# One stage of a four-layer trunk: the recurrence's first group in a fixed order, with its gate beside the value projection

## The chip, the core and the metric

The kernel runs on one core of a Trainium2 chip. The metric is device time in microseconds (us). The core has five engines that work side by side and wait for each other through semaphores: TensorE (PE, its weight loads PEld), VectorE (DVE), ScalarE (ACT), GpSimd (POOL) and SyncE (SP). SyncE and ScalarE also issue the transfers between HBM and the on-chip memory (SPq, ACTq). Each engine takes its own instructions in a fixed order. [...]

## The reference

A trunk of four layers over x and a context, 256 tokens of width 1024 each: a gated spatial layer (SGU), a bidirectional recurrent layer (RWKV-7), a latent attention layer (MLA) and a gated spatial layer again. The change lies in the recurrent layer alone. What it computes, cut to the parts that matter:

```python
r, k, v, z = (xs[e] @ w_in[e] for e in range(4))
log_w = -softplus(-(w0 + tanh(xs_w @ w_lora1) @ w_lora2)) - 0.5      # per direction n
decay = exp(-exp(log_w))
a     = sigmoid(a0 + (xs_a @ a_lora1) @ a_lora2)                      # per direction n
k_dir = k * (1 + (a - 1) * k_a)
kk    = normalize_per_head(k * k_k)
# for each token, each of 16 heads of 64, each of 2 directions:
S = S * w_t - (S @ kk_t) outer (kk_t * a_t) + v_t outer k_t
y_t = S @ r_t
out = ((norm(y_0 + y_1) + bonus(r, k_dir, v)) * silu(z)) @ w_out
```

The state is carried from the context's 256 tokens into x's 256, so the scan runs over 512 tokens.

## The kernel before

The scan is done in chunks of 64 tokens, 8 chunks, and in four groups `g` of four heads. A group has four lanes: two pairs of heads (`pr`) times two directions (`n`), lane = 2 n + pr. For each group there are these parts, each a Python generator that issues a piece of work and yields:

- `features(g)`, lane by lane (L700): the low-rank products `pw` and `pa` (L715, L716), a tanh of each on ScalarE (L730, L735), +1 on GpSimd (L731), a scan on VectorE (L739), two exponentials on ScalarE (`P` L741 and L742), then the operands of the scan's products: `AR` (L752, L753), `b` (L757), a scaling by `kab` on ScalarE (L758), and `BK`, its even rows on GpSimd (L767) and its odd rows on VectorE (L768). Their inputs k, r and kk were stored in HBM by the stage before and are fetched on SyncE's queue (L720), as are the low-rank weights (L707).
- `inverse(g)` (L778): TensorE's products `nab` (L789) and copies into `X`, a transpose on VectorE (L801), 31 pairs of dependent VectorE steps `tmp` and `Tm` (L806, L807), two transposes (L811, L813), and two rounds of small products `pg` and `px` (L826, L837).
- `operands` (`pe` L862 with its masks `E` L866, `pbk` L882) and `chain(g)` (L890): in each of 8 chunks `pz`, `pu`, `pd`, `py`, with the state `S` carried on.
- `gate(g)` (L959): the projection z as 32 products of 128x256 (`pg` L976; its tiles `xz` and `wz` tell it from the `pg` of the inverse) and a silu.

`values()` (L1068), once for the layer, is the projection of v: 64 products of 128x512 (`pv` L1076), the copy of each result (L1078), its flip in time (`prv` L1083), stores of both (L1091), and transposes (`vfm` L1096). Its weights come in four tiles `wv` of 1024 KB; two are fetched ahead of it (L1063).

Order: a scheduler places the instructions of each engine by its own costs, from the order in which the generators are interleaved. `interleave` (L115) takes from each flow in the ratio of the given numbers. The stage that the change rewrites is L1106, `values()` beside the features and the inverse of group 0; after it, the loop over `g` runs the chain of a group beside the features and inverse of the next one, the gate of its own, and the norm and output of what is done. In the trace, the stage runs from 543.4 us (first `pv`) to 656.6 us (first `pz`), the chain of group 0 to 748.6, that of group 1 to 850.8.

Tiles lie in pools: a pool with a tag has a number of buffers (`bufs`), and a tile that reuses a buffer waits until the old one was read. Pools that are closed give their space to later ones, so that tiles of two stages can lie over each other. The stage before (k and r projections) evacuates each result into a tile `ev` (L624) and stores it from ScalarE's queue (L626).

Of the kernel before, what the change touches and what calls it, by code (L numbers as in the profile page):

```python
# [8 lines left out]
F32 = mybir.dt.float32  # L9
F32R = mybir.dt.float32r  # L10
# [7 lines left out]
T = 512  # L18
# [80 lines left out]
def body(tc, I, out):  # L99
# [3 lines left out]
    V, S, PE = nc.vector, nc.scalar, nc.tensor  # L103
# [385 lines left out]
    def rwkv(m, tail):  # L489
# [182 lines left out]
        nc.gpsimd.memset(cmask[:, :, 0:1], 0.0)  # L672
        Pt = [st(f"P{i}", [128, 8, 65], 1) for i in range(2)]
# [26 lines left out]
        def features(g, f):  # L700
            f["12"] = st("12", [128, 4, 8], 3)
            for pr in range(2):
                o = g * 2 + pr
                w2 = {}
                for nm in "wa":
                    raw = st("f", [128, T], NF)[:, 0:256].rearrange("p (n c) -> p n c", n=2)
                    nc.sync.dma_start(out=raw, in_=I[f"rw_{nm}2"][:, :, o * 128:o * 128 + 128])  # L707
                    whi, wlo = st("w2" + nm, [128, 2, 128], 1, F32R), st("l2" + nm, [128, 128], 1, F32R)
# [5 lines left out]
                def second(p, nm, n):  # L714
# [3 lines left out]
                def fetch(nm, tag="f", n=NF):  # L718
                    t = st(tag, [128, T], n)
                    nc.sync.dma_start(out=t, in_=spill[nm, o])  # L720
                    return t

                ko, ro, kk = fetch("k"), fetch("r"), fetch("kk")
                kd = []
                for n in range(2):
                    lane = n * 2 + pr
                    pw = ps("pw", "f")
                    second(pw, "w", n)
                    tw = st("f", [128, T], NF)
                    S.activation(rev(tw, n), seg(pw), AF.Tanh, scale=0.5, bias=half[:, n, o:o + 1])  # L730
                    nc.gpsimd.tensor_scalar(tw, tw, 1.0, None, ALU.add)  # L731
                    pa = ps("pa", "f")
                    second(pa, "a", n)
                    ta = st("f", [128, T], NF)
                    S.activation(rev(ta, n), seg(pa), AF.Tanh, scale=0.5, bias=half[:, 2 + n, o:o + 1])  # L735
                    yield
                    c = st("f", [128, T], NF)
                    c8 = c.rearrange("p (c t) -> p c t", c=8)
                    V.tensor_tensor_scan(c, cmask.rearrange("p c t -> p (c t)"), tw, 0.0, ALU.mult, ALU.add)  # L739
                    P = Pt[n]  # L740
                    S.activation(P[:, :, 1:65], c8, AF.Exp, scale=-KAPPA2)  # L741
                    S.activation(c, c, AF.Exp, scale=KAPPA2)  # L742
                    nc.gpsimd.tensor_copy(f["12"][:, lane, :], P[:, :, 64])
                    yield

                    def r4(x):

                        return rev(x, n).rearrange("p s (c t) -> p s c t", c=4)

                    for sg in range(2):  # L750
                        ar = st(f"AR{sg}", [128, 4, 2, 64], 8)
                        V.tensor_tensor(ar[:, :, 0, :], r4(kk)[:, sg], P[:, sg * 4:sg * 4 + 4, 0:64], ALU.mult)  # L752
                        V.tensor_tensor(ar[:, :, 1, :], r4(ro)[:, sg], P[:, sg * 4:sg * 4 + 4, 1:65], ALU.mult)  # L753
                        f["AR"][lane, sg] = ar
                    yield
                    b = tw
                    V.scalar_tensor_tensor(out=seg(b), in0=seg(ta), scalar=1.0, in1=rev(kk, n), op0=ALU.add, op1=ALU.mult)  # L757
                    S.activation(ta, ta, AF.Identity, scale=half[:, 4, o:o + 1], bias=kab[:, o:o + 1])  # L758
                    yield
                    V.tensor_tensor(seg(ta), seg(ta), rev(ko, n), ALU.mult)  # L760
                    kd.append(ta)
                    b4, c4, k4 = (x.rearrange("p (s c t) -> p s c t", s=2, c=4) for x in (b, c, ta))
                    for sg in range(2):
                        bk = st(f"BK{sg}", [128, 9, 64], 8)

# [5 lines left out]
                V.tensor_tensor(seg(kd[0]), seg(kd[0]), rev(kd[1], 1), ALU.add)
                V.scalar_tensor_tensor(out=kd[0], in0=kd[0], scalar=hvec[:, 0, o:o + 1], in1=ro, op0=ALU.mult, op1=ALU.mult)
                if pr == 0:
                    spill["rk", g] = dp.tile([128, 2, T], F32, name=f"rk{g}")
# [702 lines left out]
```

## Time and profile before

| | us |
|---|---|
| median of 3 runs | 1611.42 (1608.29 to 1612.81) |
| profiled execution | 1612.92 |
| its span | 1611.1 |
| TensorE busy in the span | 1519.5 (94%) |
| VectorE, ScalarE, GpSimd busy | 1149.1, 795.2, 101.1 |
| mean granted clock of TensorE | 0.98 |

A row of the timeline gives start, length, engine, line, operation, tiles (out <- in) and how many such instructions were joined in it; in brackets the idle time of that engine just before and what ended it. A row of the windows gives, for a stretch of time, the busy time of each engine, TensorE's granted clock, the share of the transfer engines that was busy and GB/s. A 32-bit matmul leaves two records in the trace, so 16 records are 8 matmuls.

### The profile page before, as it was taken

The page shows a single profiled execution, that of the slowest core. Times are in us where ns is not written, and L with a number is a line of the kernel's source. Part 1 is how long each engine was busy: PE and PEld are TensorE (multiplying, and loading weights), DVE is VectorE, ACT ScalarE, POOL GpSimd, SP SyncE. Part 2 cuts the span into 40 slices and gives each one's busy share as a digit, 9 for nine tenths or more (in the row PEclk, how much of TensorE's full clock was granted, in tenths as well). Part 3 has the DMA queues.
Part 4 walks back from the last instruction along what each step waited for, and adds up shares of the span by engine and source line. Part 5 has one row for each costly group of instructions (what it writes and reads, how often), then busy time and mean ns, then how long its engine had stood idle before and what let it go on. Part 6 is the DMA issues. An engine that isn't in the chain of part 4 may idle for free.

```text
span 1611.1 us, 29355 instructions
## 1 busy us (share of the span) xinstructions
PE 1519.5 (94%) x11860; PEld 1181.4 (73%) x11860; DVE 1149.1 (71%) x2160; ACT 795.2 (49%) x1434; POOL 101.1 (6%) x135
## 2 busy tenths in 40 slices
PE   5999999999988998999998999799999999989998
PEld 2768888888966644776776777688777777768887
DVE  3769998864898377586887844778766666665876
ACT  4534331223665354345345332569866766356543
POOL 0000000000000132303213000000000000000000
PEclk9999999999999999899999999999999999989999
DMA  9766567742144652532433133134321222265452
GB/s 352 271 246 224 191 218 260 261 153 79 53 144 150 183 164 70 153 96 74 126 99 94 62 100 121 53 118 145 115 74 53 80 85 92 70 233 199 165 183 79
DMA packets 95176, 229.07 MB, mean 142 GB/s; under 512 B 26048, under 2 KB 52160, under 8 KB 80576
## 3 DMA queue, kind: packets, MB, share of 16 engines
q1 hardware_dynamic: 92736, 223.00, 40.8%
q10 hardware_dynamic: 2304, 4.20, 0.7%
q8 instruction: 93, 1.52, 0.4%
q14 instruction: 43, 0.35, 0.1%
HBM read 208.81 MB, written 17.83 MB: 141 GB/s over the span
## 4 chain that ended last, share of the span: by engine, by line
PE 47%; DVE 7%; ACT 5%; issue 1%; POOL 1%; DMA 0%; ACTq 0%; POOLq 0%; DVEq 0%
PE fm L323 5%; PE op L323 4%; PE pg L976 3%; PE fm L324 2%; PE op L1047 2%; PE op L324 2%; PE pz L323 2%; PE pu L323 2%; PE po L1358 2%; PE sc L1376 2%; PE pe L862 2%; PE sc L1377 1%; PE pv L416 1%; PE pv L417 1%; PE pz L324 1%
## 5 line engine op out<-in xcount | busy, mean ns | idle before, releaser
L191 DVE TENSOR_TENSOR lo<-raw,hi 128x2048 fp32r<-128x2048 f32 (+3 forms) x161 | 251.7, 1567 | 108.6 <-ACT hi L190 108.1
L190 ACT CAST hi<-raw 128x2048 fp32r<-128x2048 f32 (+3 forms) x161 | 212.1, 1324 | 226.9 <-PE op L327 40.6
L258 DVE SCALAR_TENSOR_TENSOR junk<-adaw,scb 128x1024 f32<-128x1024 f32 x112 | 136.7, 1221 | 10.0 <-DMA adaw<-in_ada_wT 8.1
L323 PE MATMUL op<-s,hi 128*128 128x512 f32 x256 | 91.6, 400 | 0.0
L415 PE MATMUL pv<-hi,hp 128*128 128x512 f32 x192 | 78.2, 409 | 9.1 <-ACT hi L190 6.0
L416 PE MATMUL pv<-lo,hp 128*128 128x512 f32 x192 | 77.7, 405 | 1.7 <-DVE lo L191 1.7
L323 PE MATMUL fm<-hx,hi 128*128 128x512 f32 x200 | 74.1, 411 | 4.1 <-ACT hx L317 3.8
L417 PE MATMUL pv<-hi,hp 128*128 128x512 f32 x192 | 77.2, 402 | 0.0
L324 PE MATMUL op<-s,lo 128*128 128x256 f32 x256 | 71.1, 280 | 0.0
L976 PE MATMUL pg<-xz,wz 128*128 128x256 f32 x256 | 70.2, 408 | 0.0
L767 POOL TENSOR_TENSOR BK<-f 64x256 f32<-64x256 f32 x64 | 57.3, 895 | 44.4 <-DVE f L760 27.4
L866 DVE TENSOR_TENSOR E<-pe,masks 128x512 f32<-128x512 f32 x64 | 41.5, 682 | 25.5 <-PE pe L862 23.0
L324 PE MATMUL fm<-hx,lo 128*128 128x256 f32 x200 | 56.7, 288 | 2.0 <-DVE lo L191 2.0
L323 PEld LDWEIGHTS op<-s,hi 128*128 128x128 f32 x256 | 48.1, 188 | 12.5 <-issue 1.3
L1076 PE MATMUL pv<-wv,xv 128*128 128x512 f32 x128 | 57.2, 596 | 0.0
L1047 PE MATMUL op<-Y,wo 128*128 128x256 f32 x192 | 55.8, 427 | 1.3 <-DVE xT L1051 1.3
L323 PE MATMUL fm<-cq,hi 128*128 128x512 f32 x144 | 55.7, 422 | 0.0
L976 PEld LDWEIGHTS pg<-xz,wz 128*128 128x128 f32 x256 | 47.0, 197 | 11.5 <-issue 3.8
L415 PEld LDWEIGHTS pv<-hi,hp 128*128 128x128 f32 x192 | 37.7, 197 | 19.4 <-ACT hi L190 6.6
L326 PE MATMUL pu<-hp,hi 128*128 128x512 f32 x128 | 51.1, 400 | 0.0
L327 PE MATMUL pu<-hp,hi 128*128 128x512 f32 x128 | 50.5, 395 | 0.0
L328 PE MATMUL pz<-hp,lo 128*128 128x512 f32 x128 | 50.5, 395 | 0.0
(413 smaller groups left out, 4088.2 us busy)
## 6 DMA issues: line engine op xcount, KB each, us to landing
adaw<-in_ada_wT SPq DMA_DIRECT2D x36, 1024.0 KB, 4.9
raw<-in_sgu_v SPq DMA_DIRECT2D x16, 1024.0 KB, 4.8
raw<-in_sgu_u SPq DMA_DIRECT2D x16, 1024.0 KB, 4.8
raw<-in_sgu_z SPq DMA_DIRECT2D x16, 1024.0 KB, 4.7
raw<-in_sgu_o SPq DMA_DIRECT2D x16, 1024.0 KB, 4.8
adaw<-in_ada_w SPq DMA_DIRECT2D x24, 512.0 KB, 9.6
xz<-xz SPq DMA_DIRECT2D x32, 256.0 KB, 4.2
raw<-in_ml_z SPq DMA_DIRECT2D x16, 512.0 KB, 3.6
```

Source lines behind the costliest of these rows:

```text
L190: S.copy(hi[:, sl], raw[:, sl])
L191: V.tensor_tensor(lo[:, sl], raw[:, sl], hi[:, sl], ALU.subtract)
L258: V.scalar_tensor_tensor(out=junk, in0=raw[:, f, :], scalar=1.0, in1=scb[:, c, :], op0=ALU.mult, op1=ALU.mult, accum_out=m[:, t * 2 + f, c ...
L323: PE.matmul(p, whi, x, start=start, stop=False)
L324: PE.matmul(p[:, 0:256], wlo, x[:, 0], start=False, stop=stop)
L415: PE.matmul(pv[tb], hs[k][:, 0, sl], whi[:, ws_], start=k == 0, stop=False)
L416: PE.matmul(pv[tb], hs[k][:, 0, sl], wlo[:, ws_], start=False, stop=False)
L417: PE.matmul(pv[tb], hs[k][:, 1, sl], whi[:, ws_], start=False, stop=k == 7)
L767: nc.gpsimd.tensor_tensor(bk[H[h], 2 * h:2 * h + 7:2, :], k4[H[h], sg], c4[H[h], sg], ALU.mult)
L976: PE.matmul(p, ws[k // 4][:, k % 4, pr * 128:pr * 128 + 128], xs[k // 2][:, k % 2, :], start=k == 0, stop=k == 7)
L1047: PE.matmul(p[:, ob], w[:, k, ob, :], y[:, k], start=k == 0, stop=k == 1)
L1076: PE.matmul(p, xv[:, k, tb * 128:tb * 128 + 128], ws[k // 4][:, k % 4, :], start=k == 0, stop=k == 7)
```

## The change

In one stage, from the first `pv` to the last product of the gate of group 0, every instruction on VectorE, ScalarE and TensorE is kept in the order in which the program writes it (`env["pin"]`). A wrapper around the three engines does that; after the stage it gives every instruction of these engines an order behind the last of the stage's third to last part, until the first part of the chain loop is written. The order is written by hand: `features` of group 0 is split into `front` (products and tanh) and `back` (the rest), the lanes come as 0, 2, 1, 3 (both directions of a pair, then of the other), and the `front` of a lane is issued one lane ahead. The gate of group 0 moves from the chain loop into this stage, into tiles of its own or of the values. `pv` is written in two halves with a yield between. The +1 is an activation on ScalarE in all 16 lanes. `v` has 6 buffers for 8, and for group 0 k, r, kk and the scan's result lie in buffers of `X` and `BK`. (In after, all calls on the three engines carry the wrapper's line, L114.)

```diff
+    class Engine:
+        def __init__(self, eng):
+            self.eng = eng
+        def __getattr__(self, name):
+            fn = getattr(self.eng, name)
+            def call(*a, **kw):
+                ins = fn(*a, **kw)
+                if env.get("pin"):
+                    tc.keep_in_program_order(ins)
+                elif self in env.get("after", ()):
+                    tc.add_manual_dep(ins.ins, env["after"][self].ins.name, mybir.DependencyInfo(
+                        mybir.DependencyClass.NoSync, mybir.DependencyReason.DATA), reason="stage order")
+                self.last = ins
+                return ins
+            return call
...
+            if g == 0:
+                x = st("X", [128, 32, 64], 2)
+                spare = [x[:, 8 * i:8 * i + 8, :] for i in range(4)] + [st("BK0", [128, 9, 64], 8)[:, 0:8, :] for i in range(4)]
+                wide = [st("BK1", [128, 9, 64], 8, F32R) for i in range(2)]
...
+            def fetch(nm, o):
+                t = spare.pop(0) if spare else st("f", [128, T], NF)
+                with tc.issue_after(state["wv"].ins):
+                    nc.sync.dma_start(out=t, in_=spill[nm, o])
+                return t
...
-                    nc.gpsimd.tensor_scalar(tw, tw, 1.0, None, ALU.add)
-                    pa = ps("pa", "f")
+                S.activation(tw, tw, AF.Identity, bias=one)
+                pa = ps("pa", "f" if g else "n")
...
         def gate(g, f):
-            ws = []
+            if g == 0:
+                w = vw.tile([128, 8, 256], F32, tag="w", name="wz", bufs=3)
+                ws = [w[:, 0:4], w[:, 4:8]]
...
+                if g == 0 and hf:
+                    xs = [vw.tile([128, T], F32, tag="v", name="v", bufs=6).rearrange("p (k t) -> p k t", k=2) for i in range(4)]
...
                         PE.matmul(p, xv[:, k, tb * 128:tb * 128 + 128], ws[k // 4][:, k % 4, :], start=k == 0, stop=k == 7)
-                    v = vw.tile([128, T], F32, tag="v", name="v", bufs=8)
+                        if k == 3:
+                            yield
+                    v = vw.tile([128, T], F32, tag="v", name="v", bufs=6)
...
-        interleave((values(), 20), (chained(features(0, fs[0]), inverse(fs[0])), 50))
+        env["pin"] = True
+        ahead, inv = chained(values(), gate(0, fs[0])), inverse(fs[0], True)
+        front, back, total, more = next(features(0, fs[0]))
+        beside(2)
+        front(0)
+        beside(2)
+        front(1)
+        back(0)
+        beside(1)
+        more()
+        front(2)
+        back(1)
...
+        next(inv)
+        beside(15)
+        interleave(islice(inv, 18))
+        for _ in range(4):
+            next(inv)
+            order = {e: e.last for e in (V, S, PE)}
+            beside(1)
+        beside(9)
+        env["pin"], env["after"] = False, order
...
-            steps, ahead, z = chain(g, f), iter(()), gate(g, f)
+            steps, ahead, z = chain(g, f), iter(()), gate(g, f) if g else iter(())
```

Three places in the order of the engines. First SyncE at the start of the stage, with the semaphores that a transfer waits for; DMAHW3 is the semaphore of a transfer queue, `f<-in_rw_w` and `f<-in_rw_a` are the low-rank weights, `vt` takes the stores of v. Before:

```order
137 L1063 DMA wv<-in_rw_v 128x2048 [waits DMAHW6_49]
138 L1063 DMA wv<-in_rw_v 128x2048 [waits DMAHW7_49]
139 L707 DMA f<-in_rw_w 128x2x128 [waits DMAHW0_49]
140 L707 DMA f<-in_rw_a 128x2x128 [waits DMAHW1_49]
141 L720 DMA f<-k_3339 128x512 [waits DMAHW2_49]
142 L720 DMA f<-r_3628 128x512 [waits DMAHW3_49,DVE_49,Activation_49]
143 L720 DMA f<-kk_3413 128x512 [waits DMAHW4_49]
144 L1063 DMA wv<-in_rw_v 128x2048 [waits DMAHW5_49]
```

And now, the same place:

```order
137 L1135 DMA wv<-in_rw_v 128x2048 [waits DMAHW6_49]
138 L1135 DMA wv<-in_rw_v 128x2048 [waits DMAHW7_49,DMAHW3_49,Activation_49]
139 L745 DMA f<-in_rw_w 128x2x128 [waits DMAHW0_49]
140 L745 DMA f<-in_rw_a 128x2x128 [waits DMAHW1_49]
141 L736 DMA X<-k_3339 128x512 [waits DMAHW2_49,PE_49]
142 L736 DMA X<-r_3628 128x512
143 L736 DMA X<-kk_3413 128x512 [waits DMAHW4_49]
144 L1135 DMA wv<-in_rw_v 128x2048 [waits DMAHW5_49]
```

The waits on ScalarE and on DMAHW3, which the fetch of r had in row 142, now stand at the second `wv` in row 138: its buffer lies over one that the last `ev` and its store of r used.

Second, VectorE at lane 0 of group 0. The row with `cmask` is the scan. Before:

```order
371 L739 SCALAR_TENSOR_TENSOR f<-cmask,f 128x512
372 L757 SCALAR_TENSOR_TENSOR f<-f 128x512
373 L752 TENSOR_TENSOR AR_4136<-f,P_4055 128x4x64
374 L753 TENSOR_TENSOR AR_4136<-f,P_4055 128x4x64
375 L752 TENSOR_TENSOR AR_4139<-f,P_4055 128x4x64
376 L753 TENSOR_TENSOR AR_4139<-f,P_4055 128x4x64
377 L768 SCALAR_TENSOR_TENSOR BK_4157<-f 128x4x64
```

And now:

```order
371 L114 SCALAR_TENSOR_TENSOR X<-cmask,f 128x512
372 L114 TENSOR_TENSOR AR_4169<-X,P_4057 128x4x64 x2
373 L114 TENSOR_TENSOR AR_4172<-X,P_4057 128x4x64 x2
374 L114 SCALAR_TENSOR_TENSOR f<-f,X 128x512
375 L114 TENSOR_TENSOR f<-f,X 128x512
376 L114 SCALAR_TENSOR_TENSOR BK_4178<-f,X 128x4x64
```

The product b (L757 before, row 374 now), behind which ScalarE's `kab` stands, has moved from ahead of the four AR products to behind them.

Third, TensorE at the end of the stage, where `pg<-xz,wz` and `pg<-v,wz` are the gate, `pz` and `pu` the first products of the chain. Before:

```order
2350 L862 MATMUL pe<-AR_4192,BK_4213 128x128
2351 L862 MATMUL pe<-AR_4136,BK_4157 128x128
2352 L862 MATMUL pe<-AR_4192,BK_4213 128x128 x2
2353 L976 MATMUL pg<-xz,wz 128x256 x4
2354 L910 MATMUL pz<-UV,E 64x64 x8
2355 L862 MATMUL pe<-AR_4284,BK_4304 128x128 x2
2356 L862 MATMUL pe<-AR_4340,BK_4358 128x128
2357 L919 MATMUL pu<-Z,X 64x64 x8
```

And now:

```order
1568 L114 MATMUL prv<-v,flip 128x512
1569 L114 MATMUL vfm<-ident,v 128x128 x16
1570 L114 MATMUL pg<-Dm,X 32x32 x32
1571 L114 MATMUL pg<-xz,wz 128x256 x4
1572 L114 MATMUL px<-X,Tm 32x32 x32
1573 L114 MATMUL pg<-xz,wz 128x256 x4
1574 L114 MATMUL pg<-Dm,X 32x32 x32
1575 L114 MATMUL pg<-xz,wz 128x256 x4
1576 L114 MATMUL px<-X,Tm 32x32 x32
1577 L114 MATMUL pg<-xz,wz 128x256 x4
1578 L114 MATMUL pg<-v,wz 128x256 x16
1579 L114 MATMUL pe<-AR_4169,BK_4178 128x128 x2
```

All 32 products of the gate of group 0 now stand ahead of its chain, where 4 stood; 16 of them fill the gaps between the rounds of the inverse, which itself follows the last values.

## Rows read from the trace of the kernel before

**Rows 1.** Windows by stage: length, busy us (count) of each engine, clock, DMA

```profile
543.40:656.60 113.20, 103.05 (x852) 54.62 (x850) 74.40 (x149) 52.50 (x95) 35.27 (x40) 0.92 0.49 139
656.60:748.60 92.00, 86.66 (x1505) 67.53 (x1506) 67.86 (x164) 39.77 (x81) 19.03 (x22) 0.96 0.32 99
748.60:850.80 102.20, 94.67 (x1590) 71.08 (x1584) 81.01 (x191) 49.19 (x96) 25.01 (x28) 1.00 0.32 100
```

**Rows 2.** Windows of 20 us at the stage's end (PE, PEld, DVE, ACT, POOL)

```profile
620.00:640.00 20.00, 14.23 (x229) 9.00 (x229) 12.51 (x26) 8.65 (x14) 3.47 (x4) 0.83 0.22 51
640.00:660.00 20.00, 17.72 (x264) 14.26 (x262) 9.76 (x18) 7.60 (x16) 5.01 (x8) 0.74 0.79 247
660.00:680.00 20.00, 16.89 (x249) 13.14 (x244) 13.81 (x27) 9.88 (x21) 6.81 (x8) 1.00 0.28 89
```

**Rows 3.** Timeline of TensorE: start, us, engine, line, operation, tiles, [idle <-releaser]

```profile
543.60 7.03 PE L1076 MATMUL pv<-wv,xv 128*128 128x512 f32 x16
...
592.36 1.08 PE L789 MATMUL nab<-AR,BK 64*32 64x64 f32 x64 [1.61 <-ACT X L794]
...
599.92 7.03 PE L1076 MATMUL pv<-wv,xv 128*128 128x512 f32 x16
...
607.76 1.13 PE L1083 MATMUL prv<-v,flip 128*128 128x512 f32 x2
...
629.84 1.92 PE L826 MATMUL pg<-Dm,X 32*32 32x32 f32 x64 [5.29 <-DVE Dm L811]
...
657.89 0.68 PE L919 MATMUL pu<-Z,X 64*64 64x64 f32 x16
...
678.72 2.13 PE L862 MATMUL pe<-AR,BK 64*128 64x128 f32 x16 [2.85 <-DVE E L866]
...
705.41 1.89 PE L976 MATMUL pg<-xz,wz 128*128 128x256 f32 x8
```

**Rows 4.** Timeline of VectorE in the inverse of group 0

```profile
596.85 1.95 DVE L801 STREAM_TRANSPOSE Dm<-X 128x1024 f32<-128x1024 f32 x1 [3.92 <-ACT X L792]
...
599.84 0.70 DVE L806 TENSOR_TENSOR tmp<-Dm,Tm 128x87 f32<-128x87 f32 x1
...
607.37 0.41 DVE L807 TENSOR_TENSOR Tm<-Tm,tmp 128x240 f32<-128x240 f32 x1
...
609.50 1.22 DVE L739 TENSOR_TENSOR_SCAN f<-cmask,f 128x512 f32<-128x512 bf16 x1
...
616.95 0.83 DVE L807 TENSOR_TENSOR Tm<-Tm,tmp 128x247 f32<-128x247 f32 x1
...
627.80 1.99 DVE L811 STREAM_TRANSPOSE Dm<-Tm 128x1024 f32<-128x1024 f32 x1
```

**Rows 5.** Timeline of GpSimd in the same stretch

```profile
599.82 1.49 POOL L731 TENSOR_SCALAR f<-f 128x512 f32<-128x512 f32 x1 [7.68 <-issue]
...
615.34 4.72 POOL L767 TENSOR_TENSOR BK<-f 64x256 f32<-64x256 f32 x4 [3.65 <-DVE f L760]
```

**Rows 6.** Chain of waits in 656.6 to 748.6, shares by line

```profile
by line: PE pg L976 14.6%; PE pe L862 8.0%; PE pd L933 4.4%; PE op L1047 3.9%; PE nab L789 3.7%; PE pz L910 3.7%; PE py L942 3.6%; DVE Tm L807 3.4%; DVE E L866 3.3%; PE pbk L882 3.1%; DVE tmp L806 3.0%; PE pg L826 2.6%; DVE f L739 2.6%; PE 
```

**Rows 7.** Timeline of ScalarE and VectorE in the first lane

```profile
550.66 0.59 ACT L1078 COPY v<-pv 128x512 f32<-128x512 f32 x1 [1.85 <-PE pv L1076]
...
555.61 0.42 DVE L752 TENSOR_TENSOR AR<-f,P 128x256 f32<-128x256 f32 x1
```

**Rows 8.** Timeline of the transfer issues of SyncE and ScalarE at the stage's start

```profile
533.88 3.60 SPq L1063 DMA_DIRECT2D wv<-in_rw_v  x2
...
544.41 0.33 ACTq L626 DMA_DIRECT2D r<-ev  x1
```

**Rows 9.** Landings of transfers issued at 544.4, 549.8 and 577.3: KB each, us

```profile
r<-ev ACTq DMA_DIRECT2D x1, 256.0 KB, 2.0
...
wv<-in_rw_v SPq DMA_DIRECT2D x1, 1024.0 KB, 8.4
...
wv<-in_rw_v SPq DMA_DIRECT2D x1, 1024.0 KB, 5.5
```

More of the change, by code (lines that the diff above doesn't have):

```diff
@@ L672, in rwkv @@
         nc.gpsimd.memset(cmask[:, :, 0:1], 0.0)
+        one = st("one", [128, 1], 1)
+        nc.gpsimd.memset(one, 1.0)
         Pt = [st(f"P{i}", [128, 8, 65], 1) for i in range(2)]
@@ L707, in features @@
                     nc.sync.dma_start(out=raw, in_=I[f"rw_{nm}2"][:, :, o * 128:o * 128 + 128])
-                    whi, wlo = st("w2" + nm, [128, 2, 128], 1, F32R), st("l2" + nm, [128, 128], 1, F32R)
+                    if pr and wide:
+                        t = wide.pop()
+                        whi, wlo = (x.rearrange(y, n=2) for x, y in ((t[:, 0:4], "p (n a) c -> p n (a c)"), (t[:, 4:6], "p n c -> p (n c)")))
+                    else:
+                        whi, wlo = st("w2" + nm, [128, 2, 128], 1, F32R), st("l2" + nm, [128, 128], 1, F32R)
                     S.copy(whi, raw)
@@ L771, in features @@
[L771 to L774, printed above, removed]
-                nc.sync.dma_start(out=spill["rk", g][:, pr], in_=kd[0])
+                pw = ps("pw", "f")
+                second(pw, "w")
+                tw = st("f", [128, T], NF)
@@ new lines, in total @@
+            def total(d):
+                o, kd = d["o"], d["kd"]
+                V.tensor_tensor(seg(kd[0]), seg(kd[0]), rev(kd[1], 1), ALU.add)
+                V.scalar_tensor_tensor(out=kd[0], in0=kd[0], scalar=hvec[:, 0, o:o + 1], in1=d["r"], op0=ALU.mult, op1=ALU.mult)
+                if d["pr"] == 0:
+                    spill["rk", g] = dp.tile([128, 2, T], F32, name=f"rk{g}")
+                nc.sync.dma_start(out=spill["rk", g][:, d["pr"]], in_=kd[0])
+            if g == 0:
+                ds, ts = [], {}
+                ds.append(operand(0))
+                fr = lambda i: ts.update({i: front(ds[i // 2], i % 2)})
+                bk = lambda i: interleave(back(ds[i // 2], i % 2, *ts[i]))
+                yield fr, bk, lambda i: total(ds[i]), lambda: ds.append(operand(1))
+                return
@@ L776, in features, with inverse @@
+            for pr in range(2):
+                d = operand(pr)
+                for n in range(2):
+                    t = front(d, n)
+                    yield
+                    yield from back(d, n, *t)
+                total(d)
                 yield
-        def inverse(f):
+        def inverse(f, first=False):
             X = f["X"] = st("X", [128, 32, 64], 2)
-            for lane in range(4):
-                pn = ps("nab", "n")
+            for j, lane in enumerate((0, 2, 1, 3) if first else range(4)):
+                pn = ps("nab", "nf"[j % 2] if first else "n")
```

133 lines of the change are left out of this document (76 added, 57 removed).

## The prediction

> **What bounds the kernel now.** I read five views of the trace of before, in this order.
>
> First, busy time by stage [rows 1]. The first row is the stage that the change rewrites, from the first value product to the first product of the chain of group 0; the next two are the chains of groups 0 and 1. TensorE is busy 103.05 of 113.20 us, then 86.66 of 92.00 and 94.67 of 102.20. No other engine is near that in the first stage (VectorE 74.40). In the two chains VectorE has 67.86 and 81.01, so TensorE bounds those too, with a few microseconds of waits.
>
> Second, the stage's clock. In the first row of [rows 1] the granted clock is 0.92; (1 - 0.92) x 113.2 = 9.1 us is what the half clock takes. So of 113.2 us some 94 are work at full clock, 9 are lost to the clock and 10 are idle. [Rows 2] place both at the end: from 620 to 660 the clock is 0.83 and 0.74, while 660 to 680, with TensorE busy only 16.89 of 20 us, has 1.00.
>
> Third, TensorE's own order of time [rows 3]. The stage has one large wait, 5.29 us before the first `pg` of the inverse at 629.84 (the wait falls into the slices with the low clock). A wait of 1.61 us before `nab` at 592.36 lies in no such slice. The waits for the long inverse and what they cost in clock are what a better order of this stage could gain.
>
> Fourth, the path behind that wait: VectorE starts the inverse with its transpose at 596.85 and ends the 31 steps at 627.80; 31 us, in which a lane of group 1 (from the scan at 609.5 on) stands between the steps, and steps of 0.41 us (607.37) become 0.83 (616.95) while GpSimd multiplies beside them (from 615.34) [rows 4, 5].
>
> Fifth, the chain of waits in group 0 [rows 6]: the gate's products are its largest part, 14.6% of 92 us, 13.4 us. These are the products that the change moves.
>
> **The change part by part.** All against the profiled execution, 1612.92 us (span 1611.1 and 1.8 around it).
>
> *The gate of group 0.* Of its 32 products (64 records) 4 stood before the first chain step; now all 32 do. 8 records (4 products) take 1.89 us with the issue pitch of full clock [rows 3], about 0.43 us a product. 28 x 0.43 = 12.0 us enter the stage and leave the chain of group 0.
>
> *Features and inverse of group 1.* By the order, the stage now holds five scans instead of six and no `nab` of group 1: 32 `nab` (1.08 us by the row at 592.36), five low-rank products (about 0.43 each, 2.1) and three `pe` less. TensorE's work in the stage: 94 + 12.0 - 1.1 - 2.1 - 0.3 = 102.5 us. The same 8.5 us leave the next two chains: the products up to group 2 sum to the same count.
>
> *Waits in the fixed order, without the transfer below.* Each engine now waits in place. (a) Six of the eight `prv` now follow their own `pv` with nothing between. From the end of `pv` at 606.95 to `prv` at 607.76 is 0.8 us [rows 3], the copy of 0.59 [rows 7] within it; for four of them, 4 us with the step to the next product. (b) On VectorE the four AR products of a lane now stand ahead of the product that `kab` on ScalarE waits for, 4 x 0.42 = 1.7 us at most, since such products overlap a little; I take 1.3 [rows 7]. The copy of `pv` stands behind `kab`, so the two others, beside the lanes, wait about 0.8 + 1.3 = 2.1 us each, 4 us. (c) The low-rank weights of the second pair are fetched behind eight stores of v; their cast and products come about 4 us late. (d) `nab` of the first lane waits for the fourth `pa` in the buffer it now shares, 1.5 us. (e) The transposes `vfm` wait for copies, 2 us. With 1.5 for smaller ones about 17 us of idle; no row has these waits, and I bound them by 6.5 (six of 0.8 and one of 1.61) and by 25 (each as long as the longest short wait, 2.85 us before `pe` at 678.72, nine times). 17 lies between, by the copies' row. The first chain product then comes at 543.6 + 102.5 + 17 = 663, a few microseconds later than before (first `pu` 657.89).
>
> *The inverse.* With the group-1 lane out of it, the 31 us shrink by its VectorE work and the steps that GpSimd doubled, to about 22. It starts later, near 603.5, since the four lanes' products stand between values. So T11 comes at about 628 as before, but TensorE has values until about 636 and doesn't wait: the 5.29 us wait and its slow clock go. That gain is already in the sum (idle and clock are counted anew).
>
> *+1 from GpSimd to ScalarE.* GpSimd took 1.49 us (599.82) [rows 5]; ScalarE's pass over the same 128x512, a copy, takes 0.59 [rows 7], and an activation is taken as 0.7. All 16 lanes change. In the long chain of a lane that is 0.8 us less, off TensorE's path; ScalarE is busy 40 to 50 of 92 to 102 us there [rows 1]. I take 0, with -2 and +2 as ends. Contention is seen in [rows 4, 5]: beside GpSimd's four multiplies of 64x256 (two inputs) steps took 0.83 instead of 0.41, beside its +1 (one input) the step of 87 columns at 599.84 took 0.70, more than one of 240 columns elsewhere. By the rows, about 0.5 us for each +1 that leaves.
>
> *A transfer that now waits.* In the order of SyncE the second `wv` transfer has gained waits on ScalarE and on queue DMAHW3: its buffer now lies over that of the last `ev`, the copy of the r projection. The store of that copy is issued at 544.41 and lands 2.0 us later, at 546.4 [rows 8, 9]. Before, both halves of `wv` were issued from 533.88 to 537.5 [rows 8] and TensorE went through all 16 records. Now 4 products (8 records, 3.4 us, half of the 7.03 in the row at 543.60) run on the first half, to 547.0; the second half starts at 546.5 and takes 5.5 us by the issue at 577, 8.4 by the one at 549.8, with k and r beside it, for 1024 KB [rows 9]. At 5.5 (nothing else moves then) it lands at 552.0: 5 us idle. Behind it in SyncE stand the low-rank weights, k, r and kk of the first pair, and behind those products in TensorE's order the rest of the stage, so nothing fills the gap. The ends are 0 (should the store not be what it waits for) and 8 us.
>
> *The clock after it.* About the wait of 5.29 us the slice 620 to 640 has a clock of 0.83 [rows 2, 3]: (1 - 0.83) x 20 = 3.4 us. The wait of 1.61 us cost nothing. I take 2, of 0 to 3.4. [...]
>
> *Sum to the first chain product:* 663 + 5 + 2 = 670, against 657.3 before (between the first `pz` and `pu`, 657.89): +12.8.
>
> *Chains of groups 0 and 1.* 8.5 us of TensorE work leave. But group 0 now holds six lanes of features where it had three: by the order, three scans, eight AR, four BK and their kin more, about 14 us, so VectorE goes from 67.86 to about 82 in a chain that TensorE could end in about 85. TensorE waits for VectorE's `E` there already (2.85 us at 678.72). I take 2.5 us back: -6, with ends -10 (all work and a wait gone) and +5 (VectorE bound). From group 2 on the order is the same.
>
> *Total:* +12.8 - 6 = +6.8 on 1612.92, 1619.7; the median of the runs shown lies 1.5 below the profiled one, so 1618. Where I rounded waits, I rounded up; I forecast 1617.
>
> **Rivals.** A change under 0.3% (4.8 us) can't be told from none by a measurement of this kernel.
>
> A, faster, the other side: the fixed order works. TensorE's waits in the stage are 8 us, near the lower bound, beside 5 for the transfer, and no clock falls; first `pu` near 543.6 + 102.5 + 8 + 5 = 659, +2; the chains are bound by TensorE and give 8.5 to 10. 1611.4 + 2 - 9 = 1604 or, with all 10 and a transfer wait of 3, 1601. For it: TensorE at 93 to 94% in the chains, and an end of the stage without the 5.29 us wait. It decides if TensorE's idle and clock losses in the stage stay under 15 us instead of 24: 657.9 - 543.6 - 102.5 = 11.8 makes the first `pu` as early as before, the chains add 8.5, and 4.8 must be left. Against it: eight `prv` in place. 20%.
>
> B, no change: the stage is 9 us later, the chains give all 8.5. 1607 to 1616. 28%.
>
> C, slower by the chain: VectorE with six lanes bounds group 0; the stage costs 12.8 and the chains give nothing or lose 4. 1611.4 + 12.8 to 1611.4 + 17 = 1624 to 1628. 17%.
>
> D, the clock swings through the stage: three of the four waits of 1.5 to 2.4 us each bring a fall like that of 620 to 640, 3.4 us each; 10 more than the forecast, 1627. By the row of 660 to 680, 5%.
>
> The forecast, 1616 to 1622 (a transfer wait of about 5 us, some 17 us of waits, the chains giving 6): 30%.
>
> That the change doesn't do what it says: the gate, the lanes and the pinned stage do stand in the order as the words have it; only that the low-rank products come early is worth little while their weights wait behind stores.
>
> **How the numbers follow.** Slower: the forecast's 30%, C's 17, D's 5: 52%. Same 28, faster 20. The range leaves 10% of A below and half of C's upper part and D above: 1601 to 1628. Alone, the forecast's own range is 1616 to 1622.
>
> **What would show it.** In the trace of after: TensorE idle of about 5 us after the first 8 records of `pv`, released by the transfer of `wv`, then a half clock; `prv` waiting on the copy each time, twice over 2 us; the first `pu` at about 670 (657.9 before); no wait above 2 us ahead of the first `pg`; the gate gone from the chain of group 0, and that stretch, first `pu` of group 0 to that of group 2, about 6 us shorter. I am wrong if the second `wv` lands in time, if the first `pu` comes before 662, or if the two chains shrink by more than 10 us.

## The result and the profile after

The changed kernel took 1630.7 us (median of 6 runs, 1626.57 to 1635.2) against 1612.12 of the kernel before on the same chip: a ratio of 1.0111 (95% interval 1.0081 to 1.0140), +17.9 us. The direction was forecast; the size, 1617 in a range to 1628, was not.

I cut both profiles at the same events: the start of the values (543.6 us) and the first state of each group's chain (the first product of `pd` with the chunk's decay on VectorE). Rows of the windows: length, busy us of PE, PEld, DVE, ACT, POOL, granted clock, DMA share, GB/s. Before:

```profile
543.60:660.20 116.60, 106.45 (x925) 57.64 (x925) 74.82 (x150) 53.93 (x98) 35.62 (x41) 0.93 0.50 142
660.20:750.60 90.40, 85.06 (x1480) 66.16 (x1478) 68.23 (x164) 39.61 (x81) 18.68 (x22) 0.96 0.29 91
750.60:852.80 102.20, 94.67 (x1590) 71.08 (x1586) 81.14 (x191) 49.19 (x96) 25.01 (x28) 1.00 0.32 100
```

After:

```profile
543.60:676.80 133.20, 115.74 (x914) 63.59 (x914) 70.97 (x142) 54.87 (x99) 20.27 (x27) 0.96 0.52 152
676.80:779.10 102.30, 93.05 (x1524) 71.31 (x1521) 86.31 (x191) 52.61 (x102) 27.05 (x32) 0.87 0.23 70
779.10:869.90 90.80, 88.01 (x1555) 67.29 (x1553) 70.85 (x173) 44.52 (x87) 14.95 (x19) 1.00 0.30 95
```

The granted clock is a share of full speed. In slices of 1 us over the whole span it is 1.00 in 1534 of 1611 slices before and in 1538 of 1627 after, 0.50 in 58 and 69, between the two in 19 and 20, and never lower; this 0.50 is what "half clock" stands for.

The stage grew by 16.6 us; the two chains together went from 192.6 to 193.1. Three numbers can be read from each row: idle (length less busy), what the half clock took, estimated as (1 - clock) x length, and the rest, work at full clock. For the two chains: work 176.1 before and 167.8 after, so about the 8.5 us of the forecast did leave; idle 12.9 and 12.0; half clock 3.6 and 13.3. By this account the half clock took back what had left, in the chain of group 0. Each kernel has one profiled execution; the lengths of its stretches are those of that one.

TensorE's timeline after, at the places of [rows 3] and at the new waits:

```profile
543.77 3.59 PE L114 MATMUL pv<-wv,xv 128*128 128x512 f32 x8
...
551.58 5.40 PE L114 MATMUL pv<-wv,xv 128*128 128x512 f32 x8 [4.22 <-DMA wv<-in_rw_v]
...
569.94 0.50 PE L114 MATMUL pw<-wx,BK 128*128 128x512 f32 x1 [1.84 <-ACT BK L114]
...
583.97 1.08 PE L114 MATMUL nab<-AR,BK 64*32 64x64 f32 x64 [1.25 <-ACT f L114]
...
590.37 1.12 PE L114 MATMUL prv<-v,flip 128*128 128x512 f32 x2 [1.68 <-ACT v L114]
...
632.46 1.13 PE L114 MATMUL prv<-v,flip 128*128 128x512 f32 x2 [0.72 <-ACT v L114]
...
673.38 0.68 PE L114 MATMUL pu<-Z,X 64*64 64x64 f32 x16
...
681.07 0.51 PE L114 MATMUL pu<-Z,X 64*64 64x64 f32 x10 [1.33 <-ACT Z L114]
...
685.03 0.48 PE L114 MATMUL pd<-UV,BKT 128*64 128x64 f32 x4 [1.29 <-DVE UV L114]
```

The second half of the first `pv` waits 4.22 us for its weights and then takes 5.40 us where the first half took 3.59. The `prv` wait for the copy, twice 1.68 and four times about 0.7. The first `pu` comes at 673.38 (657.89 in [rows 3]). The 5.29 us wait before the first `pg` is gone. The clock falls behind the transfer's wait (0.50 from 552 to 555, in the second half of `pv`), behind the waits for the second pair's weights (0.50 from 573 to 579), and again at the start and in the second half of group 0's chain (0.50 from 686 to 698 and from 733 to 746). Windows of 20 us:

```profile
560.00:580.00 20.00, 16.30 (x31) 6.53 (x31) 11.69 (x22) 9.89 (x17) 4.53 (x7) 0.83 0.33 84
...
640.00:660.00 20.00, 17.93 (x319) 14.31 (x318) 2.48 (x7) 11.39 (x20) 3.01 (x4) 1.00 0.61 175
...
680.00:700.00 20.00, 17.34 (x202) 13.06 (x202) 16.28 (x32) 11.90 (x25) 7.53 (x10) 0.66 0.27 80
...
720.00:740.00 20.00, 17.55 (x247) 13.71 (x244) 19.24 (x45) 10.37 (x19) 4.01 (x4) 0.82 0.13 40
```

The row from 640 shows that the fixed order did what it was written for at the stage's end: clock 1.00, where [rows 2] had 0.74. VectorE, though, has only 2.48 us of work there.

### The profile page after: what moved, and what is told of

It is laid out like the page before. It is cut to its first block, busy times and chain, and to the rows that moved or that the text cites. A ratio compares the mean times of both kernels' runs of the same rounds, so it can differ in the third digit from the quotient of the medians.

```text
span 1627.0 us, 29322 instructions
## 1 busy us (share of the span) xinstructions
PE 1529.2 (94%) x11860; PEld 1187.9 (73%) x11860; DVE 1153.4 (71%) x2160; ACT 805.9 (50%) x1450; POOL 79.5 (5%) x120
## 4 chain that ended last, share of the span: by engine, by line
PE 77%; DVE 12%; ACT 6%; DMA 2%; issue 2%; POOL 1%; SPq 0%; ACTq 0%; DVEq 0%; POOLq 0%
PE op L114 13%; PE pv L114 13%; PE pz L114 10%; PE pu L114 9%; PE fm L114 7%; PE sc L114 4%; PE pg L114 3%; PE pj L114 3%; PE po L114 2%; PE pe L114 1%; PE kn L114 1%; PE pm L114 1%; DVE lo L114 1%; DVE f L114 1%; DVE xs L114 1%
## 5 line engine op out<-in xcount | busy, mean ns | idle before, releaser
L114 DVE TENSOR_TENSOR lo<-raw,hi 128x2048 fp32r<-128x2048 f32 (+3 forms) x161 | 251.8, 1568 | 107.0 <-ACT hi L114 106.5
L114 ACT CAST hi<-raw 128x2048 fp32r<-128x2048 f32 (+3 forms) x161 | 212.1, 1324 | 227.1 <-PE op L114 62.8
L114 PE MATMUL op<-s,hi 128*128 128x512 f32 (+1 forms) x576 | 174.4, 371 | 0.0
L114 DVE SCALAR_TENSOR_TENSOR junk<-adaw,scb 128x1024 f32<-128x1024 f32 x112 | 136.9, 1222 | 11.4 <-DMA adaw<-in_ada_wT 9.4
L114 PE MATMUL pv<-hi,hp 128*128 128x512 f32 x384 | 124.8, 405 | 9.1 <-ACT hi L114 6.0
L114 PE MATMUL pu<-hp,hi 128*128 128x512 f32 x384 | 126.7, 398 | 0.0
L114 PE MATMUL op<-s,lo 128*128 128x256 f32 (+1 forms) x416 | 126.6, 306 | 0.0
L114 PE MATMUL pz<-hp,hi 128*128 128x512 f32 x384 | 125.5, 395 | 0.0
L114 PEld LDWEIGHTS op<-s,hi 128*128 128x128 f32 x576 | 104.0, 189 | 20.6 <-issue 1.3
L114 DVE SCALAR_TENSOR_TENSOR xT<-op,mod,xT 128x256 f32<-128x256 f32 (+1 forms) x168 | 74.5, 466 | 45.0 <-PE op L114 43.7
L114 PEld LDWEIGHTS pv<-hi,hp 128*128 128x128 f32 x384 | 75.0, 196 | 28.0 <-ACT hi L114 6.7
L114 PE MATMUL pj<-xs,hi 128*128 128x512 f32 (+1 forms) x320 | 85.6, 357 | 4.7 <-ACT hi L114 3.2
L114 PE MATMUL pz<-hp,lo 128*128 128x512 f32 (+1 forms) x256 | 86.3, 337 | 0.0
L114 PE MATMUL pu<-hp,lo 128*128 128x512 f32 (+1 forms) x256 | 86.3, 337 | 0.0
L114 PEld LDWEIGHTS pz<-hp,hi 128*128 128x128 f32 x384 | 72.0, 188 | 17.4
L114 PEld LDWEIGHTS pu<-hp,hi 128*128 128x128 f32 x384 | 71.5, 188 | 16.4
L114 PEld LDWEIGHTS op<-s,lo 128*128 128x128 f32 x416 | 78.5, 189 | 4.0
L114 PE MATMUL pv<-lo,hp 128*128 128x512 f32 x192 | 77.7, 405 | 1.7 <-DVE lo L114 1.7
L114 PE MATMUL fm<-hx,hi 128*128 128x512 f32 x200 | 73.7, 408 | 4.1 <-ACT hx L114 3.8
L114 PEld LDWEIGHTS pj<-xs,hi 128*128 128x128 f32 x320 | 56.4, 191 | 15.1 <-ACT hi L114 4.0
L114 PE MATMUL pv<-wv,xv 128*128 128x512 f32 x128 | 60.9, 625 | 4.2 <-DMA wv<-in_rw_v 4.2
L114 PE MATMUL pg<-xz,wz 128*128 128x256 f32 x224 | 59.5, 397 | 0.0
```

The lines of the kernel that those rows point to most:

```text
L114: ins = fn(*a, **kw)
```

## The experiments

Each time is a ratio to the kernel before, timed in the same rounds, times 1611 us. Each edit is shown against the kernel it starts from.

**1. The transfer's wait.** In the stage before, from the changed kernel:

```diff
 def f(o, p):
+    if nm == "k":
+        kk, sq = hk.tile(..., tag="kk", ...), hk.tile(..., tag="kk", ...)
     t = hk.tile([128, T], F32, tag="ev", name="ev", bufs=3)
...
     if nm == "k":
-        kk, sq = hk.tile(..., tag="kk", ...), hk.tile(..., tag="kk", ...)
```

> The changed kernel with one edit: in the stage before, the tiles of the normalised k are allocated ahead of the evacuation tiles, so that the second weight tile of the values lies over tiles that were read long before, and its transfer waits for no store. Theory T (the stage is long because TensorE waits in place, first of all 4.2 us for this transfer and the low clock of 540 to 580 behind it): the first pu comes 4 to 8 us earlier than the changed kernel's 673.4, and the time falls by as much, to +10 to +14 us against before. Rival (the first lane's low-rank products and their casts hold the stage anyway): the first pu moves by less than 2 us.

1.0086 (1.0056 to 1.0115), +13.9 us: 4 less than the changed kernel. In its profile the first state of group 0 comes at 667.5, 9.3 us earlier than after, and the chain of group 0 is as long as after (103.8). That profiled execution, 1619.36 us, is 6.3 below the median of its kernel, so the 9.3 is not to be taken for the gain. The wait costs about what was forecast for it, or less, and is not the whole.

**2. Less VectorE work in the chain of group 0.** From the changed kernel, AR, b, BK and the decays of group 1 are left out; group 1 reads those of group 0:

```diff
...
-for sg in range(2):
+for sg in range(2 if g != 1 else 0):
     ar = st(f"AR{sg}", [128, 4, 2, 64], 8)
...
+if g == 1:
+    for sg in range(2):
+        f["AR"][lane, sg], f["BK"][lane, sg] = fs[0]["AR"][lane, sg], fs[0]["BK"][lane, sg]
```

> The changed kernel, leaving out VectorE's and GpSimd's products for AR, b and BK of group 1 and its chunk decays (group 1 uses those of group 0), about 15 us of VectorE work less between the first product of the chain of group 0 and that of group 1; the output is not the reference's. Theory T (the chain of group 0 is held by VectorE, which has six lanes in it instead of three, and the low clock there follows from the waits): this chain shrinks from 103 us to about 91 (before: 90.5), its granted clock rises from 0.87 to 0.95 or more, the chain of group 1 keeps its 90.5. Rival G (TensorE lost the gate's products that filled its waits there, so the clock falls whatever VectorE does): the chain of group 0 stays above 99 us and its clock below 0.92.

1.0103 (1.0073 to 1.0133), +16.6 us. The chain of group 0:

```profile
679.50:782.10 102.60, 94.15 (x1513) 71.98 (x1511) 78.02 (x180) 56.47 (x109) 13.55 (x20) 0.85 0.22 67
```

VectorE is at 78.0 instead of 86.3 us and GpSimd at 13.6 instead of 27.1, and the chain is as long as before the edit, at the same low clock: Rival G's two marks. (Of the 15 us of VectorE's work only 8 fall into this chain.) So VectorE's lanes alone don't set the length, against Theory T and rival C of the prediction. But they are not off the path either. The chain of waits through this stretch, after and with the edit:

```profile
by line: DVE f L114 10.7%; POOL BK L812 9.4%; PE op L114 8.8%; PE pz L114 5.8%; DVE Tm L114 5.3%; DVE tmp L114 5.2%; DVE E L114 5.0%; issue 4.3%; PE pe L114 4.2%; DVE AR L114 4.1%; DVE Dm L114 3.9%; PE py L114 3.6%; PE pd L114 3.5%; PE pbk 
...
by line: PE op L114 9.0%; PE pz L114 7.8%; DVE f L114 6.1%; PE pe L114 6.1%; issue 5.7%; PE pa L114 5.3%; PE pbk L114 4.4%; DVE tmp L114 4.2%; DVE E L114 4.1%; PE pg L114 3.9%; DVE Tm L114 3.9%; PE nab L114 3.8%; PE py L114 3.5%; PE pu L114
```

Summed over its pieces by engine, this chain of waits is VectorE 45.4, GpSimd 9.6 and TensorE 37.0 us after (23.0, 3.2 and 53.8 before); with the edit VectorE has 31.4, GpSimd none and TensorE 58.2. Two limits of about the same length lie side by side: the lanes, and TensorE at its low clock. Where the first is shortened, the second holds.

**3. The gate back in the chain loop**, from the changed kernel:

```diff
...
-ahead, inv = chained(values(), gate(0, fs[0])), inverse(fs[0], True)
+ahead, inv = chained(values()), inverse(fs[0], True)
...
-steps, ahead, z = chain(g, f), iter(()), gate(g, f) if g else iter(())
+steps, ahead, z = chain(g, f), iter(()), gate(g, f)
```

> The changed kernel with the gate of group 0 back in the chain loop, in the chain's tiles, all else as changed. Theory T (VectorE holds the chain of group 0): the stage loses some 13 us, the first pu comes near 660, and the chain of group 0 hides the gate's 12 us in TensorE's waits: it stays at 101 to 105 us; the time falls by 10 to 13 us, to +5 to +8 against before. Rival G (the missing gate let the clock fall): the chain's clock rises to 0.95 and it keeps about 103 us with the gate in it as well: the same time. Rival P (TensorE bounds the chain): the chain grows by 10 to 12 us and the time doesn't move.

1.0113 (1.0077 to 1.0149), +18.2 us: the same time. Stage and chains of groups 0 and 1:

```profile
543.60:674.00 130.40, 108.37 (x849) 57.77 (x849) 69.27 (x138) 50.17 (x90) 22.16 (x29) 0.86 0.45 131
674.00:768.20 94.20, 87.07 (x1553) 67.61 (x1549) 77.20 (x177) 47.01 (x95) 20.03 (x24) 0.96 0.31 91
768.20:870.90 102.70, 96.39 (x1589) 71.84 (x1586) 81.12 (x191) 51.99 (x100) 18.86 (x24) 0.98 0.33 99
```

Rival G had the clock and the time; no expectation had the shorter chain. With 12 us more on TensorE the chain of group 0 is 8 us shorter, at a clock of 0.96. Not all of that is the gate's: VectorE has 77.2 us in this chain for 86.3, as work for group 2 has moved into the chain of group 1, which is 11.9 us longer than after. The two chains together are 196.9 for 193.1: 3.8 us longer with 12 us more work. And the stage, 13.7 us of products poorer, is only 2.8 us shorter: its clock falls to 0.86.

**4. No fixed order**, from the changed kernel; the scheduler places all:

```diff
-env["pin"] = True
...
-env["pin"], env["after"] = False, order
```

> The changed kernel without the fixed order: the same program text, but the scheduler places all engines' instructions in the stage as it did before, and group 1's features may move into it. Theory T (the losses come from waits in place and from group 1's lanes being kept out of the stage): the order lets group 1 start earlier; first pu at 662 to 668 (the transfer's wait of 4 us stays), two chains 184 to 190 us, +0 to +6 us against before. Rival (the moves themselves, the gate and lanes, cost it, whatever the order): +13 us or more.

1.0056 (1.0036 to 1.0077), +9.0 us, between the two expectations. The fixed order is about half of the loss. The order behind the stage goes with it; experiment 6 takes away that alone.

**5. The gate early, alone**, from the kernel before, in the tiles of the change (`v` with 6 buffers):

```diff
...
-interleave((values(), 20), (chained(features(0, fs[0]), inverse(fs[0])), 50))
+interleave((chained(values(), gate(0, fs[0])), 24), (chained(features(0, fs[0]), inverse(fs[0])), 50))
...
-steps, ahead, z = chain(g, f), iter(()), gate(g, f)
+steps, ahead, z = chain(g, f), iter(()), gate(g, f) if g else iter(())
```

> The kernel before with one part of the change: the gate of group 0 beside the values, in the tiles that the change gives it, in the scheduler's own order. Theory K (the chain of group 0 does not get shorter by the gate's 12 us, because TensorE then waits there and its clock falls): the stage ends some 8 to 10 us later, chains of groups 0 and 1 give 0 to 4 us back, +4 to +9 us against before. Rival W (the gate's products fill the 5.3 us wait and the low clock at the stage's end, and the chains give 8 or more): -3 to -8 us.

1.0083 (1.0055 to 1.0110), +13.4 us; more than Theory K asked for, since the transfer's wait comes with the tiles: TensorE waits 4.27 us for `wv`, as after. The chains:

```profile
673.00:768.30 95.30, 84.91 (x1438) 65.06 (x1439) 77.92 (x175) 43.50 (x89) 26.82 (x29) 0.89 0.27 81
768.30:869.40 101.10, 95.49 (x1564) 73.49 (x1562) 73.85 (x173) 43.89 (x87) 17.12 (x22) 0.94 0.30 94
```

196.4 us together, against 192.6 with the gate in them: 12 us of work gone, 3.8 us longer.

**6. Group 1 allowed into the stage**, from the changed kernel:

```diff
-env["pin"], env["after"] = False, order
+env["pin"] = False
```

> The changed kernel with the fixed order in the stage but without the order behind it, so that features of group 1 may move into the end of the stage, where VectorE has 18 us without work. Theory H (keeping group 1's lanes out of the stage makes the chain of group 0 long): the first pu stays near 673 or comes 1 to 3 us later, the chain of group 0 shrinks from 102.3 us to 90 to 95, the time falls by 6 to 10 us, to +8 to +12 against before. Rival K (the chain is long by its clock): the chain stays above 99 us, +15 us or more.

1.0101 (1.0038 to 1.0163), +16.3 us. In the profile the chain of group 0 went from 102.3 to 96.7, near what Theory H had, at a clock of 0.83, but the stage grew by 6.1: given back.

**7 and 8. The gate twice (7); group 2 kept behind (8).** Both from the changed kernel. The first computes the gate of group 0 again in the chain loop, unused; the second has no such products. In both, the order of VectorE keeps lanes of group 2 out of the inverse of group 1.

```diff
...
-steps, ahead, z = chain(g, f), iter(()), gate(g, f) if g else iter(())
+steps, ahead, z = chain(g, f), iter(()), gate(g, f if g else {})
```

```diff
-env["after"] = {}
+env["after"] = {V: V.last} if (g, c) == (0, 1) else {}
```

> The changed kernel with the gate of group 0 computed a second time, unused, where it stood before, in the chain loop: 32 products more on TensorE, about 13.7 us, and the scheduler keeps group 2's lanes out of the inverse of group 1, as in the next kernel. Theory K (without the gate TensorE waits in the chain of group 0 and its clock falls, which takes the 12 us back): the chain's clock is 0.95 or more against 0.87, and the chains of groups 0 and 1 together take no more than 196 us (193.1 in the changed kernel): about the same time, +15 to +20 against before. Rival P (TensorE's work bounds these chains): they grow by 10 us or more, +27 or more.

> The changed kernel with VectorE's work for group 2 kept behind that of group 0's chain, which takes two lanes of group 2 out of the inverse of group 1. Theory L (those two lanes, 10 us of VectorE between the steps of the inverse, hold the chain of group 0): that chain shrinks from 102.3 to 91 to 94 us, and the chain of group 1, which now does these lanes, grows from 90.8 to about 100: the sum stays within 3 us of 193.1. Rival K (the clock holds it): the chain of group 0 stays above 99 us and its clock below 0.90, and the sum grows by 8 us or more.

The gate twice: 1.0104 (1.0052 to 1.0156), +16.7 us, with 32 products more than the changed kernel. Group 2 behind: 1.0130 (1.0069 to 1.0192), +20.9 us. The chains of groups 0 and 1 with the gate twice:

```profile
677.40:770.10 92.70, 85.07 (x1552) 65.82 (x1550) 77.47 (x178) 45.61 (x93) 19.35 (x24) 0.98 0.31 93
770.10:870.80 100.70, 94.48 (x1586) 70.62 (x1583) 80.93 (x190) 51.99 (x100) 18.86 (x24) 1.00 0.33 101
```

And with group 2 behind, without the second gate:

```profile
676.00:773.50 97.50, 89.32 (x1500) 69.57 (x1497) 76.07 (x173) 45.52 (x91) 19.12 (x26) 0.84 0.21 59
773.50:877.20 103.70, 98.64 (x1581) 74.07 (x1579) 81.37 (x191) 50.69 (x98) 19.82 (x26) 0.93 0.32 96
```

VectorE's, ScalarE's and GpSimd's busy times in each chain are within 2 us; the one with some 13.7 us more for TensorE (32 products of 0.43: in the trace of before 4 records take 1.13 us at 711.71 and 2 take 0.70 at 715.16) has the shorter chain of group 0 by 4.8 us and the shorter sum by 7.8 us, at 0.98 instead of 0.84. The times say less: their intervals overlap, so that the second gate is shown to cost nothing that can be seen, not to gain. The chain of waits of group 0 names the limit: with the gate twice TensorE holds 26.3 of 92.7 us of it (VectorE 34.2, ScalarE 16.7), without it 66.2 of 97.5 (VectorE 20.5, ScalarE 7.4). So without the products it is TensorE, at the low clock, that this chain waits for. Theory L had the chain shorter (97.5, not the 91 to 94 asked for; Rival K's 99 was not met either), but the sum is 8.1 us above 193.1, where Rival K put it.

All 14 traces agree on the clock. In the four with all of the gate's products in it (before and experiments 3, 7 and 12) the chain of group 0 has a clock of 0.96 to 0.98; in the ten without them, or with 8 of the 32, it has 0.83 to 0.92.

**9. Fewer gate products in the kernel before.** 24 of group 0's 32 are left out:

```diff
+if g or k in (0, 7):
-PE.matmul(p, ws[k // 4][:, k % 4, pr * 128:pr * 128 + 128], xs[k // 2][:, k % 2, :], start=k == 0, stop=k == 7)
+    PE.matmul(p, ws[k // 4][:, k % 4, pr * 128:pr * 128 + 128], xs[k // 2][:, k % 2, :], start=k == 0, stop=k == 7)
```

> The kernel before with 24 of the 32 gate products of group 0 left out (the output is not the reference's); the other 8, all loads, the copies and everything else stay. 24 products are 10.3 us of TensorE. Theory K (in the chain of group 0 the gate's products cost nothing, since they stand in waits and keep the clock up): 0 to -3 us against before, the chains of groups 0 and 1 together at 189 to 194 us (192.6 before), the half clock there taking 8 us or more (3.6 before). Rival P (TensorE's work bounds the chains, as the prediction had it): -8 to -11 us.

0.9974 (0.9954 to 0.9994), -4.2 us (-7.4 to -1.0), between the two, at 4.2 of the 10.3 that were taken out. The chains:

```profile
662.30:761.90 99.60, 88.90 (x1472) 66.38 (x1467) 82.31 (x185) 48.24 (x96) 29.12 (x31) 0.91 0.31 91
761.90:853.80 91.90, 88.87 (x1554) 68.06 (x1551) 70.25 (x170) 41.07 (x82) 15.05 (x19) 0.97 0.30 94
```

191.5 us together, 1.1 less than before; the half clock takes 11.7 (0.09 x 99.6 + 0.03 x 91.9) against 3.6. So also in the kernel before, leaving these products out gives back about 4 of 10.3 us, and at most 7.4. (The clock of the stage moved as well, 0.88 for 0.93, though the stage has almost the same products; such a difference by itself proves little.)

**10 and 11. The transfer freed, with the gate early alone (10), and with the whole change but the fixed order (11).** The edit of experiment 1, on the kernels of experiments 5 and 4.

> The kernel before with the gate of group 0 early, in the scheduler's order, and the second weight tile freed of its wait as in the first experiment. Theory: of the 13 us that the gate early costs with the transfer's wait, the wait is 4 to 9, so +4 to +9 us against before; the stage grows by 5 to 8 us, the chains of groups 0 and 1 by 0 to 4. Rival (the transfer's wait is given back later): +11 us or more.

> The changed kernel without the fixed order and without the transfer's wait. Theory (fixed order about 9 us, transfer 4, the early gate the rest): +2 to +6 us against before. If the fixed order were the cause of all but the transfer: -2 to +2. If neither matters beside the gate: +9 us or more.

1.0033 (1.0018 to 1.0048), +5.3 us, and 1.0026 (1.0008 to 1.0043), +4.2 us. Both as the first expectation: the transfer's wait is 8.1 us with the gate early alone (13.4 - 5.3), 4.8 without the fixed order (9.0 - 4.2), 4.0 in the changed kernel (17.9 - 13.9); each of these has 4 to 7 us of uncertainty either way by the intervals, so that they agree. The chains of groups 0 and 1 take 194.0 us in experiment 10, against 192.6 before, and 191.2 in experiment 11, against 190.6 in experiment 12, which has the gate in them: by the estimate 13 and 10 us of work gone from TensorE, and none of it gained.

**12. The +1 on ScalarE, alone**, in the kernel before:

```diff
-nc.gpsimd.tensor_scalar(tw, tw, 1.0, None, ALU.add)
+S.activation(tw, tw, AF.Identity, bias=one)
```

> The kernel before with one part of the change: the +1 on ScalarE instead of GpSimd in all 16 lanes. Each lane gets about 0.8 us shorter and VectorE is disturbed less. If the lanes bound the chains: -2 to -6 us against before. If not, as the prediction took it: -2 to +2.

0.9964 (0.9944 to 0.9985), -5.8 us (-9.0 to -2.4): 1606.17 us (median of 10), the only version with all of the work that is faster than both kernels. VectorE's waits for what the scan needs, from 543 to 852 us, before:

```profile
DVE f L739 <- POOL f L731: 18.5, 6, 4.9
```

and with the +1 on ScalarE:

```profile
DVE f L741 <- ACT f L733: 10.7, 4, 4.8
```

VectorE's busy time in the whole run is the same (1149.1 and 1150.4 us), so the gain is not that its own steps beside GpSimd became shorter. In the stage TensorE's idle time fell from 10.1 to 5.3 us, but its clock also fell, from 0.93 to 0.87, and the stage is as long as before; the chains of groups 0 and 1 are 2.0 us shorter.

## Why the forecast was too low, step by step

**Right: the stage's start.** "At 5.5 (nothing else moves then) it lands at 552.0: 5 us idle": 4.22 us, to 551.58. The clock behind it was to cost 2: the second half of `pv` took 1.8 us longer than the first. The slice from 560 has 0.83, 3.4 us more, but that fall is not the transfer's: it stands behind the waits for the second pair's weights (1.84 and 1.38), and in experiment 1 too, where the transfer doesn't wait (eight records of `pv` take 5.25 us there, behind waits of 1.84 and 1.39). The first `pu` was to come at 670; it came at 673.38. "+12.8" for the stage was +15.5.

**Near by misses that cancel: the terms of the stage.** To the first `pu` TensorE has, by the estimates above, 107.1 us of work where the sum had 102.5, 17.5 idle where it had 22 (17 and 5), and 5.2 for the clock where it had 2:

```profile
543.60:673.38 129.78, 112.32 (x855) 60.69 (x853) 68.45 (x137) 52.80 (x96) 19.24 (x25) 0.96 0.51 147
```

**Right in kind, too large: the waits in place.** 17 us were forecast without the transfer; TensorE's idle time to the first state is 133.2 - 115.7 = 17.5 with it, 13.2 without. `prv` waits 6.2 us in all, where (a) and (b) had 8. `nab` was 1.25 for 1.5. Taking the fixed order away gives back 8.9 us with the transfer's wait (experiment 4 against the changed kernel) and 9.7 without it (experiment 1 against experiment 11); TensorE's idle time in the stage is 4.9 us less in both pairs. That the rest of the 9 us is these waits too is not shown.

**The step that failed: "Chains of groups 0 and 1 [...] -6".** They gave +0.5. The step held two ideas. The first, that work taken off TensorE shortens a chain in which TensorE is 93 to 94% busy, is wrong here: the work left (176.1 to 167.8 us), and by the estimate the half clock took 9.7 us back. In this chain the gate's products stand where TensorE would wait for VectorE or ScalarE, and with them the clock stays high (0.96 to 0.98); without them a stretch such as 680 to 700, with three waits of 0.3 to 1.33 us, has a clock of 0.66, and the products of the chain itself take up to 1.6 times as long (`pu`, 16 records: 0.68 us at 673.38, 1.12 at 697.51). Edits in both directions show it: gate put back (3), put in a second time (7 against 8), taken out early (5, 10, 11) and left out (9). The second idea, that VectorE's six lanes hold it (my "2.5 us back", rival C), is half right: the lanes make up much of the chain of waits after the change (VectorE 45.4 and GpSimd 9.6 of 102.3 us), but with 8 us of VectorE's work removed (2) the length stayed, since TensorE at a clock of 0.85 takes as long. So rival C's number, 1624 to 1628, was near by half of a mechanism; what it lacked is the clock.

**Wrong in reading [rows 2] and [rows 6].** The forecast used 660 to 680 (84% busy, clock 1.00) as evidence against rival D, as if short waits didn't cost the clock. That slice holds 16 of the gate's records; it was no test of the chain without them. And the share of the gate on the chain of waits, 14.6%, was read as time to be had. Rival D had the right kind of loss, mostly in the wrong stage: one fall came there (560 to 580, behind the wait of 1.84), but from 580 to 680 the clock after is 1.00 in each slice of 20 us, with two waits of 1.68 before `prv` in them.

**Wrong: "+1 [...] I take 0, with -2 and +2".** Alone it gives 5.8 us (12). ScalarE's +1 takes 0.72 us there (at 551.52) for GpSimd's 1.49. VectorE waited 18.5 us for GpSimd's +1 from 543 to 852, and 10.7 for ScalarE's. I had put this wait off TensorE's path; that the shorter wait is what gives the 5.8 us is likely, and no run shows it by itself.

**The sum as the runs have it.** The change without fixed order and transfer's wait: +4.2. The fixed order: 9.7. The transfer's wait: 4.0. Together +17.9, as they must be, since each is the difference of two of the runs. Within the +4.2 stand -5.8 (the +1) and +5.3 (the gate early, with its tiles); the rest, 4.7, by difference only, would be the order of lanes, the split `pv` and the borrowed buffers. It was not tried alone, and with 2 to 7 us of uncertainty on each term it is not settled. Nor is it settled why the time that VectorE has without work at the stage's end (2.5 us busy from 640 to 660) doesn't help when group 1 may use it: experiment 6 gained in the chain and lost it in the stage.

## What to carry to other kernels

Before moving work off a busy TensorE, ask what it did there: here 10.3 us of products, left out, gave back 4.2 us (experiment 9), and the chain of group 0 had a clock of 0.96 to 0.98 with all of them in it and of 0.83 to 0.92 with none, or with 8 of the 32; neither TensorE's share of busy time (93 to 94%) nor the gate's share on the chain of waits (14.6%) told that, leaving the work out in a trial did. Split a bundle of edits: here one of them alone (an addition moved from GpSimd to ScalarE) is worth 5.8 us, and the bundle cost 17.9. After changing the number or size of buffers, look at what early transfers of a stage now wait for; here one such wait cost 4 to 8 us.

## What the runs showed of the hardware that was not expected

At nearly the same busy share, the chain of group 0 ran at a clock of 0.84 with 91.6% busy (89.32 of 97.5 us, experiment 8) and at 0.98 with 91.8% (85.07 of 92.7, experiment 7). From 680 to 700 the busy time is the same, without the second gate (first row) and with it:

```profile
680.00:700.00 20.00, 18.17 (x202) 13.49 (x202) 16.39 (x32) 11.49 (x25) 7.26 (x10) 0.60 0.29 80
...
680.00:700.00 20.00, 18.17 (x255) 13.29 (x253) 16.70 (x34) 11.11 (x23) 7.58 (x10) 1.00 0.39 119
```

In the first, TensorE waits 1.32, 0.30 and 1.28 us there for `Z` and `UV`; in the second the two longest waits are 0.17 us, for `UV`, and 0.74, for a weight. The changed kernel, which has no gate products there either, has 0.66 from 680 to 700, where no wait is longer than 1.33 us. What sets the runs with the gate's products and those without apart, beyond these products, is not shown.
